# 28 of the 48 modulation chunks computed by VectorE instead of TensorE, paced by TensorE's columns

## The chip, the cores and the metric

The kernel runs on one core of one Trainium2 chip. The metric is the device time of one execution in microseconds (us). Each engine has an instruction queue of its own: TensorE (PE) multiplies, VectorE (DVE) and ScalarE (ACT) work elementwise, GpSimd (POOL) helps, and SyncE (SP) issues the transfers (DMA).

## The reference, cut to what matters

Two transformer blocks on 256 tokens (plus 256 context tokens in the first), width 1024, all in float32. The first block has two layers. Each layer derives from two condition vectors, `c` for the latent tokens and `c_ctx` for the context tokens, six vectors of 1024 numbers each, which scale, shift and gate the layer's parts:

```
for l in range(2):
    mod_l = split(silu(c)     @ ada_w[l] + ada_b[l], 6)    # ada_w[l]: 1024 x 6144
    mod_c = split(silu(c_ctx) @ ada_w[l] + ada_b[l], 6)
    hl = rms_norm(x_lat) * (1 + mod_l[1]) + mod_l[0]       # likewise hc with mod_c
    mix = mixer(hc, hl)                                    # attention, mLSTM
    x_lat = x_lat + mod_l[2] * (mix @ w_out[l])
    x_lat = x_lat + mod_l[5] * conv_ffn(rms_norm(x_lat) * (1 + mod_l[4]) + mod_l[3])
# x_ctx likewise, in layer 0 only; then the second block, without modulation
```

## The kernel before

Activations lie transposed in SBUF, features on the partitions, 512 tokens in layer 0 (context 0 to 255, latent 256 to 511). Weights come in pieces of 128 x 2048 float32 (1 MB) in the order of the list that `_plan` writes; `prefetch` loads one (`wraw`, L359, on SP's queue into a tile `raw`), and `split` makes a rounded half `whi` (ACT, L369) and a remainder `wlo` (DVE, L373). A product is three matmuls per 128 rows of depth: `mm_t` (L412 to L414, weights stationary) or `gemm_n` (L457 to L459, activations stationary).

The modulation is cut into 48 chunks (layer `l`, vector `j` of six, quarter `c` of 256 numbers), each with one 1 MB weight piece. A chunk is computed by `ada` (L500): 8 matmuls (L506; the trace shows each as two) of the two silu'd condition vectors (`sc`, 32 columns wide) with the unsplit weights, an ACT copy (L509), and 6000 columns later `fin`: two transposes on TensorE (L513) and two or three tiny DVE instructions (L515, L518, L521). The first 8 chunks (layer 0, `j` = 1 and 0) stand at the very start; `spread` puts the other 40 into the plan behind one ordinary weight piece each: 8 in the input projections of layer 0, 6 around its output projection, 19 in its feed-forward part (FFN), 6 in layer 1, and 1 in the FFN of layer 1.

`K.pipe` spaces attention units: every product calls `tick(columns)`, where a group of matmuls that pass 512 tokens by 4 x 128 rows three times counts 3 x 4 x 512 = 6144 columns, and one weight piece counts 24576 in layer 0. The instruction order on each engine's queue is not the order of the Python code: a scheduler of the language orders them when the program is built.

The consumers of modulation are `modulate` (L597: scale and shift after a norm, per 128 features DVE L602, ACT L608, POOL L609, DVE L610), the evacuation of `_wout` (L1068, `j` = 2) and of `down` in `_ffn` (L1140, `j` = 5). Layer 0's second `modulate` (`j` = 3 and 4) for the latent tokens is a list of hooks (`norm`, L589) that `_wout` calls between its last products.

Of the kernel before, what the change touches and what calls it, by code (L numbers as in the profile page):

```python
# [123 lines left out]
def _plan():  # L124
    p = []

    def cols(name, c0, cn=256, k0=0, kn=8, kind="g"):
        p.append((kind, name, k0, kn, c0, cn))

    def ada(l, j, c):  # L130
        cols(("ada_w", l), 1024 * j + 256 * c, kind=("a", l, j, c))

    def adas(l, js):
        return [(l, j, c) for j in js for c in range(4)]

    def wout(l, half):
        for n in range(2):
            cols(("w_out", l), 512 * n, 512, 4 * half, 4)

    def up(l, f0, fn):  # L140
        for s in range(fn // 2):
            cols(("ffn_up", l), 128 * f0 + 256 * s)
            cols(("ffn_up", l), DFF + 128 * f0 + 256 * s)

    def down(l, f0, fn):
        if fn == 4:
            cols(("ffn_down", l), 0, 512, f0, 4)
            cols(("ffn_down", l), 512, 512, f0, 4)
        else:
            cols(("ffn_down", l), 0, 1024, f0, 2)  # L150

    def ffn(l):
        for i, fp in enumerate(FPARTS):
            up(l, *fp)
            if i:
                down(l, *FPARTS[i - 1])
        down(l, *FPARTS[-1])

    def spread(extra, start, tail=0, skip=0):
        q = list(extra)  # L160
        body = p[start:]
        del p[start:]
        for i, x in enumerate(body):
            p.append(x)
            if i >= skip and len(q) > tail:
                ada(*q.pop(0))
        while q:
            ada(*q.pop(0))

    e = ("even_w_in", 0)  # L170
    for c in range(4):
        ada(0, 1, c)
        ada(0, 0, c)
    n = len(p)
    for c0 in (2576, 2064, 2320, 512, 768, 0, 256, 1024, 1280):
        cols(e, c0)
    spread(adas(0, (2, 4)), n)
    n = len(p)
    wout(0, 1)
    cols(e, 1536)  # L180
    cols(e, 1792)
    wout(0, 0)
    a3, a5 = adas(0, (3,)), adas(0, (5,))
    spread(a3 + a5[:2], n, 1)
    n = len(p)
    late = adas(1, (2, 4, 3, 5))
    ffn(0)
    spread(a5[2:] + adas(1, (1, 0)) + late[:9], n, 1)
    o = ("odd_w_in", 0)
    n = len(p)  # L190
    for c0 in (512, 0, 256, 1280, 768, 1792, 1536, 1024, 2048):
        cols(o, c0)
    wout(1, 0)
    wout(1, 1)
    spread(late[9:16 - 1], n, 1, 3)
    n = len(p)
    ffn(1)
    spread(late[16 - 1:], n)
    a = ("a_w_in_2", 0)
    for hg in range(4):  # L200
        for g in range(3):
            for s in range(3):
                cols(a, 3072 * g + 1024 * s + 256 * hg)
        cols(a, 9216 + 256 * hg)
    for half in range(2):
        for n in range(2):
            cols(("a_w_out_2", 0), 512 * n, 512, 4 * half, 4)
    cols(("ple_w_proj_2", 0), 0, 1024, 0, 2)
    for n in range(4):
        cols(("ple_w_gate_2", 0), 256 * n)  # L210
    b = ("b_w_in_2", 0)
    cols(b, 1024)
    for hg in range(4):
        cols(b, 256 * hg)
        cols(b, 1280 + 256 * hg)
    for half in range(2):
        for n in range(2):
            cols(("b_w_out_2", 0), 512 * n, 512, 4 * half, 4)
    cols(("ple_w_proj_2", 1), 0, 1024, 0, 2)
    for n in range(4):  # L220
        cols(("ple_w_gate_2", 1), 256 * n)
    return p
# [8 lines left out]
class _Pipe:  # L231
    def __init__(self):
        self.pending, self.live = [], []
        self.pace = 1e9
        self.credit = 0.0
        self.later = []

    def defer(self, cost, fn):
        self.later.append([cost, fn])
# [44 lines left out]
class _K:  # L284
    def __init__(self, ctx, tc, aps, out, stop=None, dbg=None):
        self.ctx, self.tc, self.nc = ctx, tc, tc.nc
        self.aps, self.out = aps, out
        self.stop, self.dbg = stop, dbg or {}
        self.plan = _plan()
        self.wi = 0  # L290
        pool = lambda n, b, **kw: ctx.enter_context(tc.tile_pool(name=n, bufs=b, **kw))
        self.cst = pool("cst", 1)
        self.raw_p = pool("raw", 2)
        self.wp = pool("whl", 4)
        self.wx = None
        self.pool_lo = 0
        self.ws = 0
        self.gi = 0
        self.wide = False
        self.pipe = _Pipe()  # L300
        self.ready = []
        self.lag = 0
        self.lookahead = 1
        self.ps = pool("ps", 2, space=bass.MemoryType.PSUM)
        self.sm = pool("sm", 6)
        self.sa = pool("sa", 2)
        self.tm = pool("tm", 6)
        self.n = 0

    def nm(self, s):  # L310
# [77 lines left out]
    def w(self):  # L388
        while True:
            self.prefetch(1)  # L390
            kind, W = self.ready.pop(0)
            self.prefetch(self.lookahead)
            if kind == "g":
                return W
            self.ada(kind, W)

    def flush_ada(self):
        while True:
# [168 lines left out]
        nc.gpsimd.tensor_tensor(rs, cs, self.mhalf[:, 0:nb], op=ALU.pow)  # L567
        return rs

    def sumsq_bcast(self, src, n, eps, square=True, rstd=True):  # L570
        st = self.stat(n)
        for k in range(KD):
            self.stat_add(st, src(k), square)
        if rstd:
            return self.stat_rstd(st, eps)
        cs = self.small([128, n // 128], "ncol")
        self.nc.vector.tensor_copy(cs, self.stat_col(st))
        return self.stat_bcast(cs, n // 128)

    def stats(self, segs):  # L580
        return {t: self.stat(b - a) for a, b, t in segs}

    def rstd(self, segs):
        t0, t1 = segs[0][0], segs[-1][1]
        return self.sumsq_bcast(lambda k: self.xt[:, k, t0:t1], t1 - t0, EPS)

    def norm(self, st, l, w, seg, h0, pad=0):
        v = {}
# [7 lines left out]
    def modulate(self, l, w, segs, H, bc, h0=0, ks=range(KD)):  # L596
        nc = self.nc  # L597
        t0, t1 = segs[0][0], segs[-1][1]
        n = t1 - t0
        for k in ks:  # L600
            xr = self.e(n)
            nc.vector.tensor_mul(xr, self.xt[:, k, t0:t1], bc)  # L602
            fu = self.e(n)
            for a, b, t in segs:
                sl = slice(a - t0, b - t0)
                A = self.mod[l][:, 3 * w + 1, t, k:k + 1]
                B = self.mod[l][:, 3 * w, t, k:k + 1]
# [326 lines left out]
def _layer0(K):  # L934
# [2 lines left out]
    segs = ((0, 256, 1), (256, 512, 0))  # L937
    with tc.tile_pool(name="h0", bufs=1) as hp, ExitStack() as es:
        H = K.H
        with tc.tile_pool(name="raw0", bufs=8) as rp:  # L940
            raw_p, K.raw_p = K.raw_p, rp
            K.prefetch(6)
            K.raw_p = raw_p
# [2 lines left out]
            K.raw_p = rp  # L946
            K.prefetch(8)
            K.raw_p = raw_p
            bc = hp.tile([128, 512], F32, name="bc0")
            nc.scalar.copy(bc, K.rstd(segs))  # L950
            K.lookahead = 0
            agw = K.split(agw, 8, 128)
            for c in range(5):
# [5 lines left out]
            K.lookahead = 1  # L959
            K.prefetch(1)  # L960
            nc.sync.dma_start(rows, K.aps["rows"].partition_broadcast(128))
        pool = es.enter_context(tc.tile_pool(name="l0", bufs=1))
        if K.stop == "h0":
            K.dump("h0", H[0].bitcast(F32)), K.dump("h0l", H[1].bitcast(F32))
# [76 lines left out]
        if K.stop == "xm0":  # L1041
            K.dump("xm0", K.xt)
            return
    return _ffn(K, 0, segs, st, K.stats)


def _ple_proj(K, pool, l):
# [11 lines left out]
def _wout(K, l, mix, segs, k0=0, parts=None, st=None, hooks=()):  # L1059
# [3 lines left out]
    def evac(m, g, lo=0, hi=512):  # L1063
        for a, b, t in segs:
# [5 lines left out]
            if st:  # L1070
                K.stat_add(st[t], x)

    for c in range(2):
        K.gemm_t(K.w(), mix, segs[-1][1] - t0, lambda m, g, *r: evac(4 * c + m, g, *r), k0, parts if c else None,
                 hooks if c else ())


def _ffn(K, l, segs, st, nxt=None):
# [3 lines left out]
    with tc.tile_pool(name=f"f{l}", bufs=1) as pool, tc.tile_pool(name=f"fw{l}", bufs=3) as wx:  # L1082
# [48 lines left out]

        def down(i, st=None):
            fn = FPARTS[i][1]

            def evac(m, g, lo=0, hi=512):
                for a, b, t in segs:
# [614 lines left out]
def _layout(i):  # L1751
    i = {k: np.asarray(v) for k, v in i.items()}
    out = {}
    kt = lambda a: np.ascontiguousarray(a.reshape(-1, 128, a.shape[-1]).transpose(1, 0, 2))
    x = np.concatenate([i["ctx"][0], i["x"][0]], 0)
    out["xt"] = kt(np.ascontiguousarray(x.T))
# [44 lines left out]
```

## Time and profile before

| | |
|---|---|
| median of 3 runs | 1669.04 us (1663.38 to 1671.32) |
| the profiled execution: its own time | 1666.1 us |
| the profiled execution: span of its instructions | 1664.3 us |
| TensorE busy | 1592.6 us |
| VectorE busy | 1127.7 us |
| ScalarE busy | 776.0 us |
| mean granted TensorE clock | 0.99 |

The span is what the rows below are measured in; 1.8 us of the execution lie outside it. Layer 0 takes the first 740 us or so: its start up to about 48 us, projections, attention and mLSTM to 340 us, FFN to 740 us. Layer 1 and its FFN end near 1134 us.

### The profile page before, as it was taken

To read this page: it belongs to the slowest core of one execution; us is meant where nothing else is said; L and a number is where in the kernel's file an instruction comes from. 1 tells how busy PE (TensorE), PEld (TensorE's weight loads), DVE (VectorE), ACT (ScalarE), POOL (GpSimd) and SP (SyncE) were. 2 spreads that over 40 slices of the span, in tenths; PEclk is the share of its full clock that TensorE was granted. 3 is DMA by queue.
4 is the path that set the end of the run, shared out by engine and by line. 5 is a ranking of instruction groups with operands and counts; after the bars stand their busy time and mean duration, and the time that the engine had idled before them with its cause. 6 is when DMAs were issued, how large, how long until landed. Compare 5 with 4: busy or idle time off the path is not lost.

```text
span 1664.3 us, 28329 instructions
## 1 busy us (share of the span) xinstructions
PE 1592.6 (96%) x11406; PEld 1385.5 (83%) x11406; DVE 1127.7 (68%) x2161; ACT 776.0 (47%) x1422; POOL 261.9 (16%) x238
## 2 busy tenths in 40 slices
PE   5899999999999999999999889999999999989998
PEld 2677776777777788878888789999999999979887
DVE  4775456575645666578677797677576666777896
ACT  3454345353323434234555455554454554545554
POOL 2221000030000000014231344441010101020111
PEclk9999999999999999999999999999999999999999
DMA  7332312434454532232333455554525243416333
GB/s 315 105 122 102 115 67 77 152 137 168 155 180 171 184 120 87 91 99 89 124 113 117 152 193 188 185 195 144 177 102 178 101 165 114 154 63 210 104 103 102
DMA packets 43475, 229.57 MB, mean 138 GB/s; under 512 B 12552, under 2 KB 15752, under 8 KB 16464
## 3 DMA queue, kind: packets, MB, share of 16 engines
q1 hardware_dynamic: 43344, 227.76, 39.4%
q8 instruction: 90, 1.47, 0.3%
q14 instruction: 41, 0.34, 0.1%
HBM read 226.70 MB, written 1.05 MB: 137 GB/s over the span
## 4 chain that ended last, share of the span: by engine, by line
PE 79%; DVE 9%; DMA 4%; POOL 3%; ACT 3%; issue 2%; SPq 0%; POOLq 0%; ACTq 0%; DVEq 0%
PE g L412 11%; PE g L413 11%; PE g L414 11%; PE g L457 6%; PE g L459 6%; PE g L458 6%; PE s L412 4%; PE s L413 4%; PE s L414 4%; DMA raw<-in_w_dram 4%; PE o L917 3%; DVE wlo L373 2%; PE t L907 2%; PE g L506 2%; POOL e L609 1%
## 5 line engine op out<-in xcount | busy, mean ns | idle before, releaser
L369 ACT CAST whi<-raw 128x1024 fp32r<-128x1024 f32 x322 | 332.0, 1048 | 282.3 <-DMA raw<-in_w_dram 172.4
L373 DVE TENSOR_TENSOR wlo<-raw,whi 128x1024 fp32r<-128x1024 f32 x289 | 356.5, 1242 | 140.7 <-ACT whi L369 132.9
L412 PE MATMUL g<-H,whi 128*128 128x256 f32 (+1 forms) x944 | 305.4, 326 | 5.1 <-ACT H L1451 1.8
L413 PE MATMUL g<-H,whi 128*128 128x256 f32 (+1 forms) x944 | 303.9, 323 | 5.1 <-DVE H L610 4.7
L457 PE MATMUL g<-whi,H 128*128 128x256 f32 x1040 | 300.8, 290 | 3.5 <-ACT H L615 2.0
L414 PE MATMUL g<-H,wlo 128*128 128x256 f32 (+1 forms) x944 | 301.5, 321 | 1.7 <-POOL wlo L371 1.7
L459 PE MATMUL g<-whi,H 128*128 128x256 f32 x1040 | 298.1, 287 | 2.9 <-DVE H L619 1.6
L458 PE MATMUL g<-wlo,H 128*128 128x256 f32 x1040 | 295.1, 284 | 0.5 <-DVE wlo L373 0.5
L457 PEld LDWEIGHTS g<-whi,H 128*128 128x128 f32 x1040 | 198.5, 191 | 11.0 <-issue 3.6
L459 PEld LDWEIGHTS g<-whi,H 128*128 128x128 f32 x1040 | 197.5, 190 | 6.5 <-DVE H L619 3.0
L412 PEld LDWEIGHTS g<-H,whi 128*128 128x128 f32 x944 | 178.2, 190 | 26.9 <-issue 4.8
L458 PEld LDWEIGHTS g<-wlo,H 128*128 128x128 f32 x1040 | 198.9, 191 | 1.1 <-DVE wlo L373 0.7
L413 PEld LDWEIGHTS g<-H,whi 128*128 128x128 f32 x944 | 179.4, 190 | 21.9 <-DVE H L610 8.8
L414 PEld LDWEIGHTS g<-H,wlo 128*128 128x128 f32 x944 | 179.1, 190 | 15.5 <-POOL wlo L371 1.9
L881 POOL TENSOR_SCALAR P<-P,rc 128x512 f32<-128x512 f32 (+2 forms) x64 | 54.7, 855 | 501.2 <-DVE rc L1612 264.1
L371 POOL TENSOR_TENSOR wlo<-raw,whi 128x1024 fp32r<-128x1024 f32 x33 | 80.9, 2453 | 103.0 <-ACT whi L369 100.1
L412 PE MATMUL s<-H,whi 128*128 128x256 f32 (+1 forms) x264 | 89.8, 340 | 0.0
L413 PE MATMUL s<-H,whi 128*128 128x256 f32 (+1 forms) x264 | 88.6, 335 | 0.0
L414 PE MATMUL s<-H,wlo 128*128 128x256 f32 (+1 forms) x264 | 88.5, 335 | 0.0
L412 PE MATMUL g<-G,whi 128*128 128x256 f32 (+1 forms) x240 | 79.4, 331 | 2.8 <-DVE e L1099 2.7
L413 PE MATMUL g<-G,whi 128*128 128x256 f32 (+1 forms) x240 | 78.3, 326 | 0.0
L414 PE MATMUL g<-G,wlo 128*128 128x256 f32 (+1 forms) x240 | 78.2, 326 | 0.0
(394 smaller groups left out, 2947.0 us busy)
## 6 DMA issues: line engine op xcount, KB each, us to landing
raw<-in_w_dram SPq DMA_DIRECT2D x209, 1024.0 KB, 4.9
xt<-in_xt_dram SPq DMA_DIRECT2D x1, 2048.0 KB
nab<-in_rpb_dram SPq DMA_DIRECT2D x16, 128.0 KB, 4.1
out_dram<-xt SPq DMA_DIRECT2D x4, 256.0 KB, 2.2
agw<-in_agw_dram SPq DMA_DIRECT2D x1, 512.0 KB, 20.7
mka<-in_tab_dram SPq DMA_DIRECT2D x1, 512.0 KB, 3.4
plr<-in_p_dram SPq DMA_DIRECT2D x2, 256.0 KB, 6.6
e<-in_tab_dram SPq DMA_DIRECT2D x5, 64.0 KB, 4.9
```

What stands on the lines that cost most here:

```text
L369: nc.scalar.copy(hi, raw)
L371: nc.gpsimd.tensor_tensor(lo, raw, hi.bitcast(F32), op=ALU.subtract)
L373: nc.vector.tensor_sub(lo, raw, hi.bitcast(F32))
L412: nc.tensor.matmul(out, hi[:, k, s], X[0][:, x], start=f, stop=False)
L413: nc.tensor.matmul(out, hi[:, k, s], X[1][:, x], start=False, stop=False)
L414: nc.tensor.matmul(out, lo[:, k, s], X[0][:, x], start=False, stop=l)
L457: nc.tensor.matmul(out, X[0][:, a + k, s], hi[:, k], start=f, stop=False)
L458: nc.tensor.matmul(out, X[0][:, a + k, s], lo[:, k], start=False, stop=False)
L459: nc.tensor.matmul(out, X[1][:, a + k, s], hi[:, k], start=False, stop=l)
L506: nc.tensor.matmul(acc[g:g + 32], self.sc[:, k, :], raw[:, k], start=(k < 4), stop=(k >= 4))
L881: nc.gpsimd.tensor_scalar(P[1], P[1], rc[:, 1:2], 0.0, op0=ALU.mult, op1=ALU.add)
L917: nc.tensor.matmul(o[64 * e:64 * e + 64], vv(e, b), u["T"][e][:, b], start=(b == 0), stop=(b == kb - 1))
```

## The change

28 chunks (`VECTOR`: layer 0's `j` = 2, 4, 3, 5, then layer 1's `j` = 1, 0, 2) leave the plan. Their weights are stored transposed in a second tensor `v`, so that 128 of the outputs lie on partitions and the 1024 inputs along the free dimension. A generator (`vector_ada`) loads each half chunk (128 x 1024, 512 KB) into one of two buffers `ar` on SP's queue and cuts it into four pieces: condition vector `t` = 0, 1 and half `h` of the inputs, each one `tensor_tensor_reduce` of 128 x 512 on VectorE that multiplies the weights by the silu'd vector (`cb`, loaded to all 128 partitions) and sums, starting from the bias or from the earlier half's sum. That makes 28 x 2 x 4 = 224 pieces. `side_step` emits one piece for each 7000 columns ticked after layer 0's first `modulate`; `need` emits at once what is still missing before a consumer is emitted. The 12 remaining chunks of layer 1 (`LATE`) stay on TensorE: 8 in layer 1 and 4 in its FFN. At the start the statistics of the first norm are made for context and latent tokens apart, and `cb` gets its silu in 512-wide instructions on ACT and VectorE.

```diff
+LATE = [(1, j, c) for j in (4, 3, 5) for c in range(4)]
+VECTOR = [(l, j, c) for l, j in ((0, 2), (0, 4), (0, 3), (0, 5), (1, 1), (1, 0), (1, 2)) for c in range(4)]
+VPACE = 7000
...
-    spread(adas(0, (2, 4)), n)
...
-    spread(a3 + a5[:2], n, 1)
...
-    spread(a5[2:] + adas(1, (1, 0)) + late[:9], n, 1)
...
-    spread(late[9:16 - 1], n, 1, 3)
+    spread(LATE[:8], n, 0, 3)
     n = len(p)
     ffn(1)
-    spread(late[16 - 1:], n)
+    spread(LATE[8:], n)
...
     def tick(self, cost):
+        if self.side:
+            self.side(cost)
...
+    def vector_ada(self):
+        nc = self.nc
+        jobs = [(l, j, 2 * c + q, n, q) for n, (l, j, c) in enumerate(VECTOR) for q in range(2)]
+
+        def fetch(i):
+            t = self.ada_p.tile([128, 1024], F32, tag="ar", name=self.nm("ar"))
+            nc.sync.dma_start(t, self.aps["v"][jobs[i][3]][:, 1024 * jobs[i][4]:1024 * jobs[i][4] + 1024])
+            return t
+
+        tiles = [fetch(0), fetch(1)]
+        yield
+        for i, (l, j, m, _, _) in enumerate(jobs):
+            raw = tiles.pop(0)
+            a0 = C_ADAB + 48 * l + 8 * j + m
+            out = self.mod[l][:, j, :, m:m + 1]
+            part = self.small([128, 2], "adr")
+            for h in range(2):
+                s = slice(512 * h, 512 * h + 512)
+                for t in range(2):
+                    nc.vector.tensor_tensor_reduce(self.e(512) if t == 0 else raw[:, s], raw[:, s], self.cb[:, t, s], 1.0,
+                                                   part[:, t:t + 1] if h else self.cols[:, a0:a0 + 1], ALU.mult, ALU.add,
+                                                   out[:, t] if h else part[:, t:t + 1])
+                    if h and t and j in (1, 4):
+                        g = C_NG + 16 * l + 8 * (j // 3) + m
+                        nc.vector.tensor_scalar(out, out, 1.0, self.cols[:, g:g + 1], op0=ALU.add, op1=ALU.mult)
+                    if h and t and i + 2 < len(jobs):
+                        tiles.append(fetch(i + 2))
+                    self.vdone = i + (h and t)
+                    yield
+
+    def side_step(self, cost):
+        self.vcredit += cost
+        if self.vcredit >= VPACE:
+            self.vcredit -= VPACE
+            next(self.vsteps, None)
+
+    def need(self, l, *js):
+        last = max((2 * n + 2 for n, x in enumerate(VECTOR) if x[0] == l and x[1] in js), default=0)
+        while self.vdone < last:
+            next(self.vsteps)
...
         n = t1 - t0
+        self.need(l, 3 * w, 3 * w + 1)
         for k in ks:
...
+            nc.sync.dma_start(K.cb.rearrange("p t k -> p (t k)"), K.aps["cb"].partition_broadcast(128))
+            K.vsteps = K.vector_ada()
+            next(K.vsteps)
...
+            for t in range(2):
+                for s in (slice(0, 512), slice(512, 1024)):
+                    sg = K.e(512)
+                    nc.scalar.activation(sg, K.cb[:, t, s], AF.Tanh, scale=0.5)
+                    nc.vector.tensor_scalar(sg, sg, 0.5, 0.5, op0=ALU.mult, op1=ALU.add)
+                    nc.vector.tensor_mul(K.cb[:, t, s], K.cb[:, t, s], sg)
+            K.pipe.side = K.side_step
...
-    return _ffn(K, 0, segs, st, K.stats)
+    st = _ffn(K, 0, segs, st, K.stats)
+    K.need(1, 0, 1, 2)
+    K.pipe.side = None
...
+    K.need(l, 2)
     for c in range(2):
...
             fn = FPARTS[i][1]
+            K.need(l, 5)
```

## Rows read from the trace of the kernel before

**Rows 1.** Windows of layer 0: length, busy PE, PEld, DVE, ACT, POOL, clock, DMA.

```profile
42.00:126.00 84.00, 76.80 (x574) 62.61 (x575) 65.82 (x150) 41.30 (x83) 22.08 (x25) 0.98 0.32 111
126.00:210.00 84.00, 84.00 (x600) 65.05 (x599) 42.44 (x109) 36.07 (x82) 7.79 (x11) 1.00 0.34 115
210.00:294.00 84.00, 81.26 (x437) 60.77 (x436) 47.49 (x140) 42.74 (x141) 4.03 (x4) 0.96 0.20 67
294.00:340.00 46.00, 45.88 (x294) 37.15 (x295) 26.88 (x57) 19.05 (x34) 0.81 (x1) 1.00 0.42 150
...
366.00:714.00 348.00, 348.00 (x1711) 272.56 (x1710) 208.01 (x322) 124.39 (x165) 0.00 (x0) 1.00 0.42 145
...
sum 714.00, PE 699.60 PEld 551.78 DVE 441.11 ACT 294.69 POOL 59.46; mean PE 99.94 PEld 78.83 DVE 63.02 ACT 42.10 POOL 8.49
```

**Rows 2.** Timeline of PE around one chunk in the FFN: start, duration.

```profile
470.45 0.39 PE L414 MATMUL s<-G,wlo 128*128 128x512 f32 x1
470.77 1.07 PE L506 MATMUL s<-raw,sc 128*32 128x256 f32 x16
...
472.11 0.40 PE L413 MATMUL g<-H,whi 128*128 128x512 f32 x1
...
474.45 0.40 PE L414 MATMUL g<-H,wlo 128*128 128x512 f32 x1
474.69 0.38 PE L513 MATMUL t<-ident,e 128*128 128x128 f32 x2
...
475.14 0.40 PE L413 MATMUL g<-H,whi 128*128 128x512 f32 x1
```

**Rows 3.** Windows of the chunks' matmuls alone (L506): length, busy PE, PEld.

```profile
126.00:210.00 84.00, 5.51 (x64) 1.89 (x64) 1.00 0.34 115
...
294.00:340.00 46.00, 3.60 (x56) 1.54 (x60) 1.00 0.42 150
...
366.00:580.00 214.00, 18.20 (x272) 7.10 (x272) 1.00 0.49 170
```

**Rows 4.** Timeline of PE: the last chunk of layer 0 and what follows.

```profile
740.32 1.07 PE L506 MATMUL g<-raw,sc 128*32 128x256 f32 x16
742.89 0.39 PE L457 MATMUL g<-whi,H 128*128 128x256 f32 x1 [1.50 <-ACT H L608]
```

**Rows 5.** DVE groups by shape: count, busy us, mean ns, idle before.

```profile
L373 DVE TENSOR_TENSOR wlo<-raw,whi 128x1024 fp32r<-128x1024 f32 x289 | 356.5, 1242 | 140.7 <-ACT whi L369 132.9 <-PE g L414 6.2
...
L1609 DVE CUSTOM_DVE_ANT_0 e<-s,mka 128x512 f32<-128x512 f32 x32 | 21.8, 687 | 11.3 <-PE s L1606 11.3
L1480 DVE TENSOR_TENSOR e<-e,e 128x512 f32<-128x512 f32 x24 | 16.5, 686 | 0.1
...
L1609 DVE DVE_READ_ACCUMULATOR2_ANT nb<- 128x1 f32 x32 | 2.6, 83 | 0.0
```

**Rows 6.** Timeline of DVE: two such pairs back to back.

```profile
1230.98 0.68 DVE L1609 CUSTOM_DVE_ANT_0 e<-s,mka 128x512 f32<-128x512 f32 x1
...
1231.66 0.69 DVE L1609 CUSTOM_DVE_ANT_0 e<-s,mka 128x512 f32<-128x512 f32 x1
```

**Rows 7.** Single lines on DVE: ns min/median/max, first and last start us.

```profile
L691 DVE TENSOR_SCALAR nid<-ident x1: 174/174/174, 3.9 to 3.9; 36x36 f32<-36x36 f32 x1
...
L1090 DVE TENSOR_SCALAR hw<-cols x2: 211/216/222, 316.0 to 928.5; 128x66 f32<-128x66 f32 x2
...
L602 DVE TENSOR_TENSOR e<-xt,t x40: 412/415/422, 339.7 to 937.5; 128x256 f32<-128x256 f32 x40
L602 DVE TENSOR_TENSOR e<-xt,bc x8: 680/684/960, 28.3 to 42.8; 128x512 f32<-128x512 f32 x8
```

**Rows 8.** DMA issues: KB each, median us from issue to landing.

```profile
mka<-in_tab_dram SPq DMA_DIRECT2D x1, 512.0 KB, 3.4
```

**Rows 9.** Windows of 3 us after a wait of PE, columns as in Rows 1.

```profile
63.00:66.00 3.00, 1.52 (x13) 0.97 (x13) 2.75 (x10) 1.57 (x4) 0.00 (x0) 1.00 0.00 0
66.00:69.00 3.00, 2.86 (x19) 1.11 (x19) 2.92 (x8) 0.00 (x0) 0.00 (x0) 0.57 0.00 0
```

More of the change, by code (lines that the diff above doesn't have):

```diff
@@ L176, in _plan @@
         cols(e, c0)
-    spread(adas(0, (2, 4)), n)
-    n = len(p)
     wout(0, 1)
@@ L182, in _plan @@
     wout(0, 0)
-    a3, a5 = adas(0, (3,)), adas(0, (5,))
-    spread(a3 + a5[:2], n, 1)
-    n = len(p)
-    late = adas(1, (2, 4, 3, 5))
     ffn(0)
-    spread(a5[2:] + adas(1, (1, 0)) + late[:9], n, 1)
     o = ("odd_w_in", 0)
@@ L236, in __init__ @@
         self.later = []
+        self.side = None
     def defer(self, cost, fn):
@@ L307, in __init__ @@
         self.tm = pool("tm", 6)
+        self.ada_es = ctx.enter_context(ExitStack())
+        self.ada_p = self.ada_es.enter_context(tc.tile_pool(name="ada", bufs=2))
+        self.cb = self.ada_p.tile([128, 2, 1024], F32, tag="cb", name="cb", bufs=1)
+        self.vsteps, self.vdone, self.vcredit = None, 0, 0.0
         self.n = 0
@@ L568, in stat_pow, with rstd @@
         return rs
[L570 to L578, printed above, removed]
     def stats(self, segs):
         return {t: self.stat(b - a) for a, b, t in segs}
-    def rstd(self, segs):
-        t0, t1 = segs[0][0], segs[-1][1]
-        return self.sumsq_bcast(lambda k: self.xt[:, k, t0:t1], t1 - t0, EPS)
+    def rstd(self, segs, out):
+        sts = self.stats(segs)
+        for a, b, t in segs:
+            for k in range(KD):
+                self.stat_add(sts[t], self.xt[:, k, a:b])
+            self.nc.scalar.copy(out[:, a:b], self.stat_rstd(sts[t], EPS))
     def norm(self, st, l, w, seg, h0, pad=0):
@@ L939, in _layer0 @@
         H = K.H
-        with tc.tile_pool(name="raw0", bufs=8) as rp:
+        with tc.tile_pool(name="raw0", bufs=8) as rp, tc.tile_pool(name="bc0", bufs=1) as bp:
             raw_p, K.raw_p = K.raw_p, rp
@@ L948, in _layer0 @@
             K.raw_p = raw_p
-            bc = hp.tile([128, 512], F32, name="bc0")
-            nc.scalar.copy(bc, K.rstd(segs))
+            nc.sync.dma_start(K.cb.rearrange("p t k -> p (t k)"), K.aps["cb"].partition_broadcast(128))
+            K.vsteps = K.vector_ada()
+            next(K.vsteps)
+            bc = bp.tile([128, 512], F32, name="bc0")
+            K.rstd(segs, bc)
             K.lookahead = 0
@@ L1043, in _layer0 @@
             return
-    return _ffn(K, 0, segs, st, K.stats)
+    st = _ffn(K, 0, segs, st, K.stats)
+    K.need(1, 0, 1, 2)
+    K.pipe.side = None
+    K.ada_es.close()
+    return st
 def _ple_proj(K, pool, l):
@@ L1753, in _layout @@
     out = {}
+    out["cb"] = np.concatenate([i["c"][0], i["c_ctx"]])
     kt = lambda a: np.ascontiguousarray(a.reshape(-1, 128, a.shape[-1]).transpose(1, 0, 2))
@@ L1781, in _layout @@
     out["w"] = w
+    out["v"] = np.stack([i["ada_w"][l][:, 1024 * j + 256 * c:1024 * j + 256 * c + 256].T.reshape(2, 128, 1024)
+                         .transpose(1, 0, 2).reshape(128, 2048) for l, j, c in VECTOR])
     out["tab"] = _tables()
```

## The prediction

> **What bounds the kernel now.** I read the busy times first. TensorE is busy for 1592.6 of the 1664.3 us, VectorE for 1127.7; so on average TensorE is the bound, but an average says nothing about the place that the change touches. I therefore cut layer 0 into windows [rows 1]. The reader is to see two things there. From 126 to 210 us, from 294 to 340 and from 366 to 714 TensorE is busy all the time, so work taken from it there shortens the kernel. And VectorE, which is to take the work, is busy for 441 of the 714 us from 42 to 756: 273 us are idle. They are spread unevenly: from 42 to 126 us it is busy for 65.8 of 84 us and TensorE already waits for 7 us there, while in the FFN it is busy for 208 of 348.
>
> Next I read the timeline of TensorE around one chunk, to price it where TensorE is full, then where the chunks stand, then VectorE's groups for the price of a piece, and last the single lines that tell in which order a queue is filled.
>
> **What leaves TensorE.** In the FFN one matmul of a 512-token product starts 0.234 us after the one before (ten such steps from 472.11 to 474.45) [rows 2]. From 470.45 to 472.11 there are two steps and a chunk: 1.66 - 0.47 = 1.19 us. From 474.45 to 475.14 there are two steps and the chunk's two transposes: 0.69 - 0.47 = 0.22 us. A chunk costs 1.41 us where TensorE is full, and 28 of them 39.5 us; that is the most that can be gained on TensorE.
>
> Not every chunk stands where TensorE is full. A chunk is 16 of the L506 matmuls. 272 of them, 17 chunks, stand between 366 and 580 us; 64 stand in 126 to 210 us, which is 4 chunks; 56 stand in 294 to 340 us, that is 4 chunks, the last cut by the window's end [rows 3]. These 25 give 25 x 1.41 = 35.3 us. The remaining 8 of layer 0's 33 stand where TensorE has waits, and some fill them: after the one at 740.32 TensorE still waits 1.50 us for the next norm [rows 4], so taking it away gives nothing. Between 0 and 1.41 us each I take the middle, 0.7 us: 5.6 us (0 to 11.3).
>
> Layer 0 loses 33 chunks and only 28 leave TensorE: layer 1 and its FFN have 12 instead of 7. Three of the five new ones land in the full FFN, 4.2 us, and two in layer 1 at 0.7 us: -5.6 us. The ACT copies and tiny VectorE instructions of the 28 go too; nothing waits for them. Net on TensorE: 35.3 + 5.6 - 5.6 = **35 us less** (30 to 39.5).
>
> **What comes to VectorE.** 224 pieces of 128 x 512. The trace has the same operation pair with other arithmetic, a product-and-reduce of 128 x 512 from PSUM and SBUF (687 ns) followed by a read of the accumulator (83 ns); a plain two-operand instruction with both operands in SBUF takes 686 ns [rows 5]. Back to back, one pair starts 0.68 us after the other [rows 6]. What the trace does not show is this operation with both streams from SBUF. The nearest rows bound it: 0.68 us, and 1.242 us for a two-operand instruction of twice the width plus the 0.083 us read, 1.33 us, if it took two steps per element. I take 0.68 us, since both 686 and 687 ns rows lie there. 224 x 0.68 = 152 us, against 273 us of idle time; if all of it could be used, nothing would be late.
>
> When do they run? Counted by the ticks, 15 weight pieces x 24576 columns pass before layer 0's second norm: 368640 / 7000 = 52 pieces paced, and one more is forced by `_wout`. That norm needs 12 chunks, 96 pieces, so `need` emits 43 at once in front of it. Later the paced rate suffices: 4 are forced at the first `down`, 8 at the end of layer 0. But emission is not execution. VectorE ran `nid`, written inside the mLSTM gates, at 3.9 us, before any projection, and the FFN's `hw`, written behind the norm that starts at 339.7 us, at 316.0 us [rows 7]. Instructions whose inputs are there are drawn forward into idle time. The pieces depend on nothing but their own transfer and the piece before. So I take it that they fill VectorE's idle time from the first moments on. From 42 to 340 us that is 298 - 182.6 = 115 us [rows 1], and the 96 pieces need 65 us. A burst of 43 in front of the norm should not remain.
>
> The loads: 56 halves of 512 KB replace 28 of 1 MB. One lands 3.4 us after issue [rows 8], and with two buffers the next half of 4 x 0.68 = 2.7 us is worked off meanwhile; since pieces get less than half of VectorE's time, a half takes over 6 us and hides its successor. They queue on SP among the weight loads, but DMA is busy for only 20 to 42% of these windows [rows 1].
>
> **What the pieces cost.** A piece that has started is not interrupted, so an instruction that TensorE waits for comes late by up to 0.68 us, 0.34 on the mean. Where TensorE is full, three to five accumulators in PSUM hide that. It shows where a chain of small steps goes through VectorE: two norms around 340 us with 8 steps each (16 x 0.34 = 5.4 us, half hidden by products: 3), the attention from 42 to 126 us (TensorE's waits of 7 us grown by half: 3), four mLSTM heads with three steps each (12 x 0.34: 4, of which 3 count). Together **9 us**. Below, 0, if all is hidden; above, 35 us, where it would eat the gain: that is 23% of the pieces' 152 us.
>
> At the start, the silu of `cb` puts 8 instructions of at most 0.68 us (5.4 us) on VectorE in front of the first projections, and the halved norm statistics add 8 x (2 x 0.41 - 0.68) = 1.1 us by the two widths of L602 [rows 7]. Between 0 and 6.5 us I take **2**, as ACT and TensorE alternate with VectorE there and leave gaps.
>
> Sum: -35 + 9 + 2 = -24 us. The profiled execution took 1666.1 us (1664.3 in the span, 1.8 around it), so 1642 us. The median of the runs is 2.9 us above it, 1645 on that scale; I predict 1643.
>
> **Rivals.** *The price is hidden less well.* VectorE then has no gap left until about 400 us, and each late step reaches TensorE. For it: from 63 to 69 us VectorE is nearly full and TensorE waits, and behind such a wait the granted clock fell to 0.57 for 3 us [rows 9]. Against it: TensorE's full windows. At 30 us instead of 9 the time is 1663: no change that can be told (within 0.5%, 8 us, is about what a measurement here cannot tell from none).
>
> *The emission order holds on VectorE, and the change makes it slower.* The 43 pieces stand in front of the norm, TensorE has nothing to do meanwhile. A half then takes (2.7 + 3.4)/2 = 3.1 us, since two buffers give one load per two halves: 10.75 x 3.1 = 33 us, 5 us for the 8 pieces in front of layer 1, 2 us for the clock after the wait; with the start and 5 us of lateness 47 us, so +12: 1678. It decides from 35 us of waiting on. Against it stand [rows 7].
>
> *A piece takes twice as long.* At 1.33 us the 224 pieces need 298 us and do not fit in 273; before the second norm 96 need 128 us of 115. TensorE would wait at least 13 us there and 12 more later, and with only four fifths of the idle time usable (218 us) 80 us in all: 1666 - 35 + 80 = 1711. [...]
>
> **How the numbers follow.** Forecast 0.62 (1630 to 1655); hidden less well 0.18 (1655 to 1672, a third of it still faster); emission order 0.12 (1668 to 1685, half slower, half the same); double price 0.08 (above 1680). Faster by over 0.5%: 0.62 + 0.06 = 0.68; slower: 0.06 + 0.08 = 0.14; within: 0.18. The range leaves out the double price, the upper half of the emission order and a few in a hundred below: 1628 to 1677.
>
> **What would show it.** Right: the FFN's weight pieces follow each other 1.4 us sooner; pieces of about 0.69 us scattered over 45 to 450 us; no gap on TensorE near 330 us. Wrong: a run of some 40 pieces in front of L602 with TensorE idle; a piece above 1.1 us; waits of TensorE for VectorE that sum to over 30 us before 400 us; pieces waiting for their loads with other VectorE work behind them.

## The result and the profile after

The changed kernel took 1692.08 us (median of four runs, 1691.64 to 1698.14) against 1667.18 us before: 1.0153 times as long, 95% interval 1.0124 to 1.0182. It is slower by 25 us where 24 us less had been forecast. The profiled execution is the longest of the four, 1698.14 us with a span of 1696.4 us; it is compared below with the span of before, 1664.3 us, so the stages add up to 32 us.

First the page's engine line. TensorE has indeed less to do (1567.0 us busy, 1592.6 before), and VectorE more:

```profile
PE 1567.0 (92%) x10902; PEld 1383.0 (82%) x10902; DVE 1272.6 (75%) x2577; ACT 768.5 (45%) x1407; POOL 266.7 (16%) x239
```

So the loss is waiting: TensorE is busy for 26 us less, and its span is 32 us longer. The windows of layer 0, as in [rows 1], tell where: length, then busy PE, PEld, DVE, ACT, POOL, granted clock, DMA.

```profile
42.00:126.00 84.00, 73.74 (x499) 63.40 (x498) 75.99 (x170) 42.71 (x81) 21.77 (x22) 0.94 0.30 99
126.00:210.00 84.00, 84.00 (x587) 67.95 (x586) 51.98 (x143) 34.12 (x82) 8.10 (x13) 1.00 0.29 96
210.00:294.00 84.00, 81.50 (x396) 61.12 (x396) 57.33 (x166) 45.97 (x145) 4.41 (x4) 0.96 0.16 52
294.00:336.00 42.00, 33.11 (x194) 28.64 (x192) 38.02 (x92) 17.05 (x29) 1.89 (x2) 0.91 0.41 140
336.00:378.00 42.00, 7.57 (x37) 6.98 (x38) 33.10 (x90) 6.78 (x11) 7.58 (x10) 0.52 0.48 159
378.00:714.00 336.00, 335.78 (x1482) 274.08 (x1481) 274.79 (x519) 121.83 (x156) 6.00 (x7) 1.00 0.40 133
```

Up to 294 us and in the FFN TensorE is as busy as before, but for 3 us in the first window; between 336 and 378 us it is busy for 7.57 of 42. The waits of TensorE from 42 to 400 us (engine, line, releaser: total, times, longest) and its timeline show one hole:

```profile
PE g L457 <- ACT H L647: 36.6, 1, 36.6
PE t L600 <- POOL nrs L612: 4.2, 1, 4.2
```

```profile
332.51 1.22 PE L600 MATMUL t<-ident,nrs 128*128 128x128 f32 x4 [4.16 <-POOL nrs L612]
370.30 0.58 PE L457 MATMUL g<-H,whi 128*128 128x256 f32 x1 [36.57 <-ACT H L647]
```

L647 is the scale and shift that follows L641 (L602 before). The first L641 of the second norm, at 339.7 us before [rows 7], now starts at 369.2:

```profile
L641 DVE TENSOR_TENSOR e<-xt,t x40: 408/415/421, 369.2 to 956.7; 128x256 f32<-128x256 f32 x40
```

What stands in front of it is pieces. The windows of L420, the pieces alone (busy VectorE; two instructions are one piece, the product and the accumulator's read):

```profile
42.00:84.00 42.00, 3.69 (x9) 0.88 0.37 123
84.00:126.00 42.00, 7.41 (x21) 1.00 0.22 76
126.00:168.00 42.00, 12.73 (x36) 1.00 0.35 114
168.00:210.00 42.00, 0.00 (x0) 1.00 0.23 79
210.00:252.00 42.00, 0.00 (x0) 0.98 0.15 51
252.00:294.00 42.00, 7.76 (x21) 0.94 0.17 53
294.00:336.00 42.00, 14.82 (x41) 0.91 0.41 140
336.00:378.00 42.00, 23.97 (x68) 0.52 0.48 159
```

Some 33 pieces are done by 168 us, then none at all for two windows, although VectorE is idle for 32 of 84 us from 126 to 210; then the rest in a heap: 36 pieces (72 instructions) between 331.6 and 369.3 us. Where the pause ends is seen on VectorE's timeline:

```profile
269.42 0.69 DVE L745 TENSOR_TENSOR e<-t,trif 128x512 f32<-128x512 f32 x1 [1.80 <-PE t L743]
270.28 0.69 DVE L745 TENSOR_TENSOR e<-t,trib 128x512 f32<-128x512 f32 x1 [0.17 <-PE t L743]
270.89 0.74 DVE L420 CUSTOM_DVE_ANT_0 e<-ar,cb,cols 128x512 f32<-128x512 f32 x1
```

L745 makes the mask tiles `md` of the mLSTM heads; these two are the last head's. They lie in the ring `e` of six buffers, and so do the throw-away products of half of the pieces (`self.e(512)` for `t` = 0). The first piece after the pause comes right behind the last `md`. This gave the theory for the experiments: the ring's buffers go to those who ask in the order in which the code asks; a piece written behind the heads gets its buffer only after them.

A table by stage, from the first or last start of single lines, carries the comparison (us; the columns are the kernels of the experiments below). The marks are: first product of layer 0's projections; first evacuation of `_wout`; first L641 of the second norm; first convolution of the FFN; first `rr` in layer 1's attention; last evacuation of layer 1's `_wout`; first tile of the second block; end of the span. The row `layer 1` therefore holds layer 0's FFN and also the first steps of layer 1 up to its first `rr` (in the kernel before, the last chunk of the FFN starts at 740.32 us and that `rr` at 792.3); it is called the FFN row below.

| stage up to | before | after | e1 | e3 | e5 | e6 |
|---|---|---|---|---|---|---|
| first projection | 48.7 | 51.2 | 53.5 | 49.2 | 50.2 | 53.3 |
| first `_wout` | 176.3 | 167.9 | 169.9 | 167.4 | 169.6 | 168.2 |
| second norm | 114.7 | 150.1 | 107.2 | 147.6 | 104.2 | 105.2 |
| FFN begins | 20.9 | 18.3 | 17.4 | 16.5 | 18.3 | 17.7 |
| layer 1 | 431.7 | 414.1 | 406.9 | 423.7 | 413.0 | 407.2 |
| layer 1's `_wout` done | 135.4 | 140.9 | 140.6 | 136.8 | 138.2 | 135.7 |
| second block | 206.5 | 220.5 | 220.2 | 206.5 | 206.4 | 200.2 |
| end | 530.1 | 533.4 | 531.9 | 531.2 | 532.1 | 532.7 |
| span | 1664.3 | 1696.4 | 1647.6 | 1678.9 | 1632.0 | 1620.2 |

After against before: +2.5 at the start, -8.4, then +35.4 in the stage of the hole, -2.6, -17.6 in the FFN row, and another +5.5 and +14.0 in layer 1 and its FFN, +3.3 in the second block: 32.1 us. There are two losses, not one.

### The profile page after: what moved, and what is told of

Its sections match the earlier page's. It is cut to its first block, busy times and chain, and to the rows that moved or that the text cites. A ratio compares the mean times of both kernels' runs of the same rounds, so it can differ in the third digit from the quotient of the medians.

```text
span 1696.4 us, 27786 instructions
## 1 busy us (share of the span) xinstructions
PE 1567.0 (92%) x10902; PEld 1383.0 (82%) x10902; DVE 1272.6 (75%) x2577; ACT 768.5 (45%) x1407; POOL 266.7 (16%) x239
## 3 DMA queue, kind: packets, MB, share of 16 engines
q8 instruction: 86, 1.41, 0.3%
## 4 chain that ended last, share of the span: by engine, by line
PE 74%; DVE 11%; DMA 5%; POOL 3%; issue 3%; ACT 2%; SPq 0%; POOLq 0%; DVEq 0%; ACTq 0%
PE g L457 10%; PE g L459 10%; PE g L458 10%; PE g L502 6%; PE g L504 6%; PE g L503 6%; PE s L459 4%; PE s L457 4%; PE s L458 4%; DMA raw<-in_w_dram 3%; PE o L956 3%; DVE wlo L377 3%; PE t L946 2%; POOL e L648 2%; PE s L819 1%
## 5 line engine op out<-in xcount | busy, mean ns | idle before, releaser
L377 DVE TENSOR_TENSOR wlo<-raw,whi 128x1024 fp32r<-128x1024 f32 x289 | 360.5, 1251 | 110.5 <-ACT whi L373 109.4
L457 PE MATMUL g<-H,whi 128*128 128x256 f32 (+1 forms) x912 | 296.7, 327 | 45.1 <-ACT H L647 37.7
L458 PE MATMUL g<-H,whi 128*128 128x256 f32 (+1 forms) x912 | 296.0, 325 | 2.7 <-DVE H L649 2.0
L459 PE MATMUL g<-H,wlo 128*128 128x256 f32 (+1 forms) x912 | 293.3, 323 | 3.4 <-POOL wlo L375 3.4
L457 PEld LDWEIGHTS g<-H,whi 128*128 128x128 f32 x912 | 173.7, 191 | 61.5 <-ACT H L647 38.3
L502 PEld LDWEIGHTS g<-whi,H 128*128 128x128 f32 x1040 | 200.9, 194 | 11.5 <-ACT whi L373 3.0
L504 PEld LDWEIGHTS g<-whi,H 128*128 128x128 f32 x1040 | 200.0, 193 | 5.3 <-DVE H L658 3.1
L458 PEld LDWEIGHTS g<-H,whi 128*128 128x128 f32 x912 | 174.2, 191 | 19.8 <-DVE H L649 5.0
L459 PEld LDWEIGHTS g<-H,wlo 128*128 128x128 f32 x912 | 174.2, 191 | 17.2 <-POOL wlo L375 3.8
L920 POOL TENSOR_SCALAR P<-P,rc 128x512 f32<-128x512 f32 (+2 forms) x64 | 53.5, 836 | 497.5 <-DVE rc L1667 264.0
L459 PE MATMUL s<-H,wlo 128*128 128x256 f32 (+1 forms) x296 | 99.3, 336 | 1.7 <-POOL wlo L375 1.7
L457 PE MATMUL s<-H,whi 128*128 128x256 f32 (+1 forms) x296 | 99.6, 337 | 1.1 <-ACT whi L373 1.1
L458 PE MATMUL s<-H,whi 128*128 128x256 f32 (+1 forms) x296 | 99.5, 336 | 0.0
L375 POOL TENSOR_TENSOR wlo<-raw,whi 128x1024 fp32r<-128x1024 f32 x33 | 80.8, 2449 | 115.1 <-ACT whi L373 115.1
```

The source lines that it names most:

```text
L375: nc.gpsimd.tensor_tensor(lo, raw, hi.bitcast(F32), op=ALU.subtract)
L377: nc.vector.tensor_sub(lo, raw, hi.bitcast(F32))
L457: nc.tensor.matmul(out, hi[:, k, s], X[0][:, x], start=f, stop=False)
L458: nc.tensor.matmul(out, hi[:, k, s], X[1][:, x], start=False, stop=False)
L459: nc.tensor.matmul(out, lo[:, k, s], X[0][:, x], start=False, stop=l)
L502: nc.tensor.matmul(out, X[0][:, a + k, s], hi[:, k], start=f, stop=False)
```

## The experiments

Every ratio is to runs of the kernel before on the same chip, with its 95% interval. The edits are to the changed kernel.

**e1, own tile.** The throw-away products leave the ring.

```diff
-  nc.vector.tensor_tensor_reduce(self.e(512) if t == 0 else raw[:, s], ...
+  nc.vector.tensor_tensor_reduce(self.junk() if t == 0 else raw[:, s], ...
...
+    def junk(self):
+        return self.ada_p.tile([128, 512], BF16, tag="aj", name=self.nm("aj"), bufs=1)
```

> One part changed: the pieces that wrote their products into a tile of the shared ring `e` write them into a tile of their own (128 x 512, bf16; the products are thrown away, the sums stay float32). Theory A (the ring holds the pieces back: its six buffers are handed out in the order in which the code asks, so a piece written behind the mLSTM heads cannot start before the heads have got theirs; 35 pieces were left over and TensorE waited 36.6 us for them in front of the second norm): the pieces run earlier, some 70 before the first output projection instead of 32, the wait falls from 36.6 us to under 8 us, and the time falls by 25 to 33 us to 1660-1668. Rival B (the emission order itself binds the pieces on VectorE): the wait stays above 30 us and the time within 5 us of 1692.

Measured: 1644.58 us (1643.52 to 1649.42), ratio 0.9881 (0.9854 to 0.9907): 47 us below the changed kernel, and 15 us below what was expected. Of the 48.8 us between the two spans in the table, 42.9 lie in the row of the hole and 7.2 in the FFN row, where none had been expected. In TensorE's waits from 42 to 400 us the 36.6 us are gone; the longest is now

```profile
PE t L597 <- DVE st L590: 2.9, 1, 2.9
```

and the windows of the pieces (L420 as above) show them where VectorE had been idle (some 72 pieces before 210 us, 33 in the changed kernel):

```profile
126.00:168.00 42.00, 16.81 (x44) 1.00 0.40 126
168.00:210.00 42.00, 25.39 (x69) 1.00 0.54 165
210.00:252.00 42.00, 13.12 (x37) 0.96 0.36 119
252.00:294.00 42.00, 17.48 (x48) 0.92 0.34 109
294.00:336.00 42.00, 7.54 (x20) 0.95 0.30 101
336.00:378.00 42.00, 9.55 (x26) 0.97 0.46 163
```

That TensorE does not suffer from it is in the windows of all engines: with VectorE at 79.26 of 84 us TensorE stays full.

```profile
126.00:210.00 84.00, 84.00 (x586) 68.47 (x587) 79.26 (x227) 34.94 (x82) 8.15 (x13) 1.00 0.47 146
```

The tile is bf16 instead of float32; the pieces take as long (744 to 749 ns mean for each form, 746 to 747 before the edit), so that is not where the time went.

**e8, the heads' tiles out of the ring instead.** The counter-test: pieces stay in the ring.

```diff
-        md = K.e(512)
+        md = pool.tile([128, 512], F32, tag="md", name=K.nm("md"), bufs=1)
...
-    junk = pool.tile([128, 128], F32, tag="junk", name=K.nm("junk"), bufs=2)
+    junk = pool.tile([128, 128], BF16, tag="junk", name=K.nm("junk"), bufs=1)
```

> The pieces stay in the shared ring e, and instead the eight tiles md of the mLSTM heads get a buffer of their own; one write-only scratch tile of the heads is cut to bf16 in one buffer to make room. Theory A (it is the ring as such that holds the pieces, whoever asks for its buffers next: behind md come the tanh tiles of the heads' output gate and the squares of the statistics, which wait as long): only the five buffers' worth, 10 pieces, starts earlier, the heap in front of the second norm stays, and the time is that of the changed kernel within 10 us, 1682 to 1695 us, with a wait of TensorE of 25 to 37 us there. Rival B (the heads' md tiles alone held them): about what the own tile for the pieces gave, 1640 to 1655 us, with no wait over 5 us there.

Measured: 1692.0 us (1688.39 to 1694.83), ratio 1.0148 (1.0111 to 1.0185): the same as the changed kernel. TensorE still waits for 35.8 us,

```profile
PE g L457 <- ACT H L647: 35.8, 1, 35.8
```

and the pause only begins later, at 178 us. VectorE's timeline (two separate rows) has no piece between

```profile
177.18 0.75 DVE L420 CUSTOM_DVE_ANT_0 ar<-ar,cb,cols 128x512 f32<-128x512 f32 x1
...
292.03 0.74 DVE L420 CUSTOM_DVE_ANT_0 e<-ar,cb,adr 128x512 f32<-128x512 f32 x1
```

and ScalarE's timeline shows what precedes the second of them, the next claimant of the ring, the tanh tiles of the heads' output gate:

```profile
282.92 0.62 ACT L1076 ACTIVATE e<-g 128x512 f32<-128x512 f32 x1
291.14 0.59 ACT L1076 ACTIVATE e<-g 128x512 f32<-128x512 f32 x1
```

So `md` was only the first in line. My first wording of the theory, that the heads held the pieces, falls; that the ring does, whoever stands in it, holds.

**e2, one piece per 3500 columns**, in the changed kernel with its ring.

```diff
-VPACE = 7000
+VPACE = 3500
...
-        if self.vcredit >= VPACE:
+        while self.vcredit >= VPACE:
```

> One part changed: a piece for each 3500 columns instead of 7000, two where one tick brings enough credit. 105 pieces are then emitted in front of the second norm, 96 are needed. Theory A and rival B alike: no burst, TensorE's wait there falls from 36.6 us to under 8 us, time 1660-1670. Theory C (VectorE as a whole is too full in layer 0, wherever the pieces stand): the wait moves to the attention or to the heads, and the time stays above 1680.

Measured: 1658.44 us (10 runs, 1656.6 to 1663.61), ratio 0.996 (0.9946 to 0.9975). That is 1.6 us below the range of theory A and rival B. From 42 to 400 us the longest single wait of TensorE is 2.8 us. The pieces still pause, though for a shorter time: by the windows of L420 there are 40 instructions from 168 to 210 us, none from 210 to 252. Writing twice as many ahead of the claimants is a way around the ring, and nearly as good at the hole itself; it does not beat e1.

**e7, both: own tile and 3500 columns.** The two edits of e1 and e2 together.

> Own tile, and one piece for each 3500 instead of 7000 columns. Theory A (what held the pieces was the shared ring, and with it out of the way the order in which they are written no longer decides, since VectorE draws them forward as it is idle): the same as the own tile at 7000 within 6 us, 1639 to 1651 us. Rival B (the pace has its own part in the loss, as the 34 us that it gave with the shared ring could mean): 1615 to 1632 us. Rival C (pieces drawn in too thickly delay the splits and statistics ahead of TensorE): 1655 us or more.

Measured: 1652.54 us (1647.64 to 1656.32), ratio 0.99 (0.9877 to 0.9923). 1.5 us above theory A's bound and far from B: with the ring out of the way a denser pace gains nothing. It may cost something: the medians lie 8 us apart, but against their own runs of before e1 and e7 differ by 3 us (0.9881 and 0.99), within both intervals. The pace mattered in e2 only because of the ring. In the stretch from 294 to 378 us TensorE is busy for 77.91 of 84 us, against 79.92 in e1, 2 us less; I did not place more.

**e4, two vectors back on TensorE.** Layer 0's `j` = 4 and 3 return to the plan; 20 chunks, 160 pieces.

```diff
-VECTOR = [... ((0, 2), (0, 4), (0, 3), (0, 5), (1, 1), (1, 0), (1, 2)) ...]
+VECTOR = [... ((0, 2), (0, 5), (1, 1), (1, 0), (1, 2)) ...]
...
+    spread(adas(0, (4,)), n)
+    n = len(p)
...
+    spread(adas(0, (3,)), n)
```

> One part undone: the 8 chunks that the second norm waits for (layer 0, vectors 4 and 3) are on TensorE again, among the projections and around the output projection as before; 20 chunks stay with VectorE. Only 32 pieces are then due before the second norm. Theory A and B: no burst, the wait of 36.6 us goes, 8 chunks cost up to 11 us on TensorE again: 1667-1672. Theory C (VectorE too full in general): the time falls by less than 15 us, above 1677.

Measured: 1656.42 us (9 runs, 1652.38 to 1661.35), ratio 0.9945 (0.9925 to 0.9965); longest wait of TensorE before 400 us 3.3 us. Without demand in front of the second norm there is no heap. It came out some 11 us better than expected. Part of that is the FFN row, which takes 404.8 us here (from the first convolution at 360.8 to the first `rr` at 765.6), 9 us less than in the changed kernel and 2 less than in e1, with 160 pieces instead of 224.

**e3, the other 12 chunks where they were before.** 5 in layer 0's FFN, 6 in layer 1, 1 in its FFN.

```diff
+    n = len(p)
     ffn(0)
+    spread(LATE[:5], n, 1)
...
-    spread(LATE[:8], n, 0, 3)
+    spread(LATE[5:11], n, 1, 3)
...
-    spread(LATE[8:], n)
+    spread(LATE[11:], n)
```

> One part changed: the 12 chunks that stay on TensorE stand where the kernel before had its last 12: 5 in layer 0's FFN, 6 in layer 1, 1 in layer 1's FFN, instead of 0, 8 and 4. The burst stays. Theory D (from layer 0's end to the end of layer 1's FFN the changed kernel loses 16 us against before: chunks there cost more than 1.41 us, since their 1 MB loads and the loads of the weights share two buffers in a stage that waits for weights): 5 x 1.41 = 7 us more in layer 0's FFN and some 15 us less afterwards, so 8 us less, 1684. Rival E (a chunk costs 1.41 us wherever it stands, and the loss comes from elsewhere): the time within 3 us of 1692.

Measured: 1682.38 us (1680.72 to 1683.58), ratio 1.0101 (1.0078 to 1.0125): 10 us below the changed kernel, with the hole (35.6 us) untouched. The table says which stage: layer 1 -4.1 us for two chunks fewer, its FFN -14.0 us for three fewer, the FFN row +9.6 us for five more. That is theory D; rival E is out. Whether D's reason, two buffers shared by two kinds of loads, is the right one is taken up below.

**e5, own tile and the 12 chunks as before.** The edits of e1 and e3.

> Both mends at once: the pieces' throw-away products go into a tile of their own, and of TensorE's 12 remaining chunks 5 lie in the first feed-forward, 6 in layer 1 and 1 in the second feed-forward, as in the kernel before, instead of 0, 8 and 4. Each alone gave 47 us (own tile) and 10 us (chunks as before). Theory A, the two losses lie in different stages and add: from the first mend's 1644.6 us, the first feed-forward longer by about 9 us (5 chunks), layer 1 and the second feed-forward shorter by 18 us, together 1633 to 1638 us. Rival B, the crowded second feed-forward was only late because everything ahead of it was, so the own tile has already bought it back: 1642 to 1652 us, since 5 more chunks then stand in a stretch where TensorE is full.

Measured: 1635.67 us (1633.79 to 1640.82), ratio 0.9806 (0.9784 to 0.9828). The losses add.

**e6, own tile and 36 chunks.** Layer 1's `j` = 4 and 3 join the queue; TensorE keeps four, in layer 1, none in its FFN.

```diff
-LATE = [(1, j, c) for j in (4, 3, 5) for c in range(4)]
+LATE = [(1, j, c) for j in (5,) for c in range(4)]
-VECTOR = [... (1, 1), (1, 0), (1, 2)) ...]
+VECTOR = [... (1, 1), (1, 0), (1, 2), (1, 4), (1, 3)) ...]
...
-    spread(LATE[:8], n, 0, 3)
+    spread(LATE, n, 0, 3)
...
-    spread(LATE[8:], n)
...
-    K.need(1, 0, 1, 2)
+    K.need(1, 0, 1, 2, 3, 4)
```

> Own tile, and 36 instead of 28 chunks on VectorE: the 8 for layer 1's norms and gates after its input projections follow in the queue, 64 more pieces; TensorE keeps 4, all in layer 1. Theory A (a chunk costs TensorE 1.9 us in the first feed-forward, 2.5 us in layer 1, near 4.7 us in the second, and VectorE's idle time takes 64 pieces of 0.72 us, 46 us of the some 52 us that it has free between 546 and 714 us): about 18 us below the own tile alone for the 4 chunks gone from the second feed-forward and 10 us for 4 gone from layer 1, so 1616 to 1630 us. Rival B, VectorE becomes the bound at the end of the first feed-forward (84 us stretches with 56.5 us of its other work): its splits come late, TensorE waits there, and 10 us or more of it is lost again: 1632 to 1650 us.

Measured: 1620.48 us (1618.97 to 1622.0), ratio 0.971 (0.9693 to 0.9726): the best kernel of the study, 48 us below the one before.

**e9, own tile and all 40.** `j` = 5 of layer 1 too, `LATE` is empty.

> Own tile, and all 40 chunks behind the start on VectorE, 320 pieces; TensorE keeps none, and all must be done by the end of the first feed-forward. Theory A (TensorE is the bound in layer 1 as well, and VectorE's idle time still takes them): 4 chunks fewer in layer 1 at 2 to 2.5 us, 1608 to 1614 us. Rival B (VectorE is full: with 288 pieces it was busy 79 to 81 of 84 us in two stretches of the first feed-forward and 72.65 in the third, so of the 23 us of the 32 added pieces some 10 to 20 us are left over in front of layer 1, where TensorE waits for them): 1618 to 1635 us, with a run of pieces and a wait there.

Measured: 1639.68 us (1637.06 to 1641.21), ratio 0.9838 (0.9809 to 0.9866), 19 us above e6. Theory B has the place right, and the size there: the first `rr` of layer 1 moves from 751.6 to 770.2 us, 18.6 us. The total lies 4.7 us above its range. The four chunks fewer in layer 1 gave back only 3.9 us (131.8 us up to the last evacuation of `_wout`, 135.7 in e6), and layer 1's FFN took 3.5 us more (203.7 against 200.2). The windows of all engines:

```profile
672.00:714.00 42.00, 39.49 (x221) 34.76 (x220) 38.09 (x99) 14.02 (x29) 8.44 (x10) 0.88 0.27 98
714.00:756.00 42.00, 28.43 (x172) 24.72 (x171) 35.91 (x91) 15.90 (x27) 18.91 (x17) 0.78 0.40 122
```

The last 19 pieces run in the second window (e6 has its last at 678 us), and TensorE is idle there for 13.6 us. It is not one hole but many short waits: after 700 us 7.1 us in five for ScalarE's and 5.5 us in seven for VectorE's part of the norm.

## Why the prediction was wrong, point by point

**The step that failed** is the sentence "The pieces depend on nothing but their own transfer and the piece before", and with it "A burst of 43 in front of the norm should not remain". Half of the pieces also depend on a buffer of the ring `e`, which the projections' and the heads' own work holds in the order of the code. The rows on which I leaned [rows 7], `nid` and `hw` drawn forward, show instructions that write tiles of their own; they could not show what an instruction does that asks for a shared buffer. e1 takes the ring away and finds the forecast drawing-forward: 198 instructions of pieces from 126 to 294 us, 57 in the kernel with the ring.

**The rival "emission order"** had the symptom nearly right, 33 us for 43 pieces; measured was a wait of 36.6 us with 36 pieces in 37.7 us. Its reason was only half right: emission order does not hold on VectorE in general (e1), but through the ring it did. Its price for a half chunk, 3.1 us, was low; in the heap the starts of every second half on VectorE's timeline are 347.23, 355.55 and 363.44 us, so (363.44 - 347.23) / 4 = 4.05 us for a half, with VectorE waiting for loads:

```profile
355.55 0.75 DVE L420 CUSTOM_DVE_ANT_0 e<-ar,cb,cols 128x512 f32<-128x512 f32 x1 [1.79 <-DMA ar<-in_v_dram]
...
363.44 0.75 DVE L420 CUSTOM_DVE_ANT_0 e<-ar,cb,cols 128x512 f32<-128x512 f32 x1 [1.42 <-DMA ar<-in_v_dram]
```

These waits sum to 6.9 us there, where I had said that a half hides its successor; that was said for spread pieces, and in e1 they are 3.4 us in the whole kernel. The waits are not all of it: from 331.6 to 369.3 us VectorE is busy for 29.89 us, 25.38 of them with pieces and the rest with other work between them. The rival's 1678 us was 14 us too low all the same, mainly because it shared the forecast's price for the five chunks (below).

**The price of a piece** was right. VectorE's groups by form and two neighbours in the heap:

```profile
L420 DVE CUSTOM_DVE_ANT_0 e<-ar,cb,cols 128x512 f32<-128x512 f32 x56 | 41.8, 747 | 6.9 <-DMA ar<-in_v_dram 6.9
```

```profile
351.53 0.75 DVE L420 CUSTOM_DVE_ANT_0 ar<-ar,cb,cols 128x512 f32<-128x512 f32 x1
352.20 0.08 DVE L420 DVE_READ_ACCUMULATOR2_ANT adr<- 128x1 f32 x1
352.20 0.75 DVE L420 CUSTOM_DVE_ANT_0 e<-ar,cb,adr 128x512 f32<-128x512 f32 x1
```

One starts 0.67 us after the other, as assumed (0.68), though a single one is shown as 747 ns instead of the 687 of [rows 5]. The rival "twice as long" is refuted: both sources are float32 in SBUF and the step is 0.67 us; no run shows its 1.33 us, an estimate from an instruction of twice the width [rows 5].

**TensorE's gain in layer 0** was right in size, but only once the hole is gone. Forecast were 35.3 + 5.6 = 40.9 us without lateness; e1 gains 6.4 + 7.5 + 3.5 + 24.8 = 42.2 us by the table between the first projection and layer 1. The price of 1.41 us [rows 2] holds. In the kernel before, 320 of the L506 matmuls, 20 chunks, ran in the row "FFN begins" and the FFN row together. In these two rows e1 gains 3.5 + 24.8 = 28.3 us, 1.4 for each; the five chunks that e5 puts back cost 0.9 + 6.1 = 7.0 us, 1.4 each, and those of e3 7.8 us, 1.6 each. In the changed kernel the FFN row gives 17.6 us, 7.2 less than in e1. TensorE's waits in this row add up to 13.1 us there and to 6.1 in e1, so they are 7.0 of the 7.2. All 13.1 come between 742 and 785 us, at the norm in front of layer 1 and in the first steps behind it. The changed kernel's last 18 pieces run at that norm (714 to 758 us; e1 has its last at about 554) and are the likely cause, for which the rival "emission order" had 5 us; no run isolates them.

**Lateness, +9 us**, was over-sized. After 42.2 us of gain against 40.9 forecast next to nothing is left for it: even if all 33 chunks had been worth 1.41 us, 46.5 in all, it would be 4.3 us. From 126 to 210 us e1's VectorE is busy for 79.26 of 84 us, and TensorE is full. That a started piece is not interrupted is shown only so far that each of the changed kernel's 224 took 729 to 757 ns (e1: 730 to 772, but for one of 1115); that it is the accumulators in PSUM that hide a late step, no run isolates. "Hidden less well" fell with it. It reappears in e9, when VectorE has little slack at the FFN's end (busy for 38.09 of 42 us from 672 to 714).

**The start, +2 us**: right on the mean. The nine kernels and the changed one begin their projections at 49.2 to 53.5 us, 51.4 on the mean, against 48.7; e1 is the latest of them, 4.8 us behind the kernel before.

**Five more chunks in layer 1 and its FFN, -5.6 us**, was mis-sized by a factor of three: 18.9 us from the first `rr` of layer 1 to the second block (360.8 in e1, 341.9 before), and 343.3 in e3, which has the old number. The two in layer 1 were near the mark (8, 6 and 4 chunks: 140.6, 138.2 and 135.7 us, 1.2 each). The three in its FFN cost not 1.41 but 4.6 us each (4 and 1 chunks: 220.2 and 206.4 us; with none, in e6, 200.2). TensorE's timeline around one of them in e1 shows why the price from layer 0's FFN could not be carried over:

```profile
929.17 1.07 PE L554 MATMUL s<-raw,sc 128*32 128x256 f32 x16
930.89 0.38 PE L460 MATMUL s<-H,whi 128*128 128x256 f32 x1 [0.65 <-ACT whi L373]
931.11 0.28 PE L461 MATMUL s<-H,whi 128*128 128x256 f32 x1
931.24 0.28 PE L460 MATMUL g<-H,whi 128*128 128x256 f32 x1
931.36 0.28 PE L461 MATMUL g<-H,whi 128*128 128x256 f32 x1
933.34 0.39 PE L462 MATMUL s<-H,wlo 128*128 128x256 f32 x1 [1.70 <-POOL wlo L375]
```

Here a matmul passes 256 tokens and the next starts 0.12 us later, half of what it is in layer 0's FFN (0.234 us, from [rows 2]). The same weights feed TensorE for half as long, and a chunk that takes a place in the row of weight loads leaves TensorE waiting for `whi` and then for `wlo`: 929.17 to 933.34 are 4.17 us, in which four ordinary matmuls (0.5 us) ran. The `wlo` waited for is one that GpSimd makes in 2.37 us (L375), where VectorE's take 1.24 on the mean of the whole kernel. This wait of 1.7 us occurs three times in this stage of e1 (4 chunks), once in e5 and in the kernel before (1 chunk) and never in e6 (none). Behind the first of e1's three the granted clock is low as well: 0.55 from 922.0 to 925.5 us, with 17 matmuls, where 29 run in the 3.5 us from 933.3, behind the second, at a clock of 1.00. The loads stand behind the chunks too, as theory D of e3 has it: SP waits with a weight load until TensorE has worked off a chunk for 28.9 us in this stage of e1 (27.8 in the changed kernel), 13.6 in e5 (13.6 in the kernel before) and 0 in e6. That the supply of weights has no margin in this stage is argued from these rows and from the counts of chunks; it was not tried by itself, and neither was a kernel whose remainders VectorE makes there. The number of tokens alone does not set the price: layer 1's output projection, too, passes 256, and layer 1's chunks cost 1.2 us.

**In sum**: the changed kernel stands 47 us above e1, which is the ring's price. e1 ends at 1644.6 us, 1.6 from the forecast of 1643, partly by chance: some 9 us of lateness that hardly came pay for most of the 13 us by which the five chunks were under-priced, and its own runs of before (1665.8 us) lie below the 1669.04 from which the forecast was made, so that its gain is 21 us where 24 had been forecast.

## What to carry to other kernels

Before work is counted as fit for idle time, list every buffer that it asks for, and who asks for the same buffers between its place in the code and the time at which it should run: here a write-only result in a shared ring tied it to that order as hard as a data dependency (a wait of TensorE of 36.6 us), and a tile of its own freed it (the longest is 2.9 us in e1). And a price read in one stage has to be read again in the next: the same chunk cost 1.4 us in layer 0's FFN, 1.2 in layer 1 and 4.6 in layer 1's FFN, where TensorE stopped for split weights behind it. When moving work has paid, ask for the last piece that still fits: 36 chunks on VectorE gave 1620 us, 40 gave 1640.

## What the hardware showed that I had not expected

The multiply-and-sum of 128 x 512 with both float32 sources in SBUF and the accumulator's read behind it ran at one start per 0.67 us, no slower than the form with one source in PSUM (0.68 us [rows 6]), while its single duration is shown 60 ns longer (747 against 687).

The granted clock behind the wait of 36.57 us, by windows of all engines (columns as in the first windows above): 0.50 in the first 4 us of matmuls, a mean of 0.70 in the next 4, and 1.00 from 378 to 714 us. By an estimate from these counts that adds at most 3.5 us to the wait: 38 matmuls run in the 8 us from 370 to 378, where 68 would at the 34 of the next 4 us; the norm's own steps hold back some of them too.

```profile
370.00:374.00 4.00, 3.57 (x13) 2.98 (x14) 3.57 (x11) 2.65 (x5) 3.75 (x5) 0.50 0.63 211
374.00:378.00 4.00, 4.00 (x25) 4.00 (x26) 3.34 (x10) 2.73 (x5) 3.63 (x6) 0.70 0.02 4
378.00:382.00 4.00, 4.00 (x34) 3.80 (x33) 3.48 (x10) 2.68 (x5) 3.70 (x5) 1.00 0.00 0
```
